# Row halves and banks of the head products and low-rank products in a recurrence's preparation

## The chip, the cores and the metric

One core of one Trainium2 chip runs the whole program. The metric is the device time of one execution in microseconds (us), median over runs.

## The reference

Two layers of a transformer block work on 512 tokens and 256 context tokens of width 1024. Each layer mixes two groups: differential attention over 8 heads, and a gated linear recurrence (RWKV-7) over 8 heads of 64 channels that runs once forwards and once backwards. An output projection and a wide perceptron with a squared ReLU follow. The change touches the inputs of the recurrence. Cut to that:

```python
def direction_terms(k, kk, xw, xa, w0, w_b, a0, a_b, k_a):
    wl = (w0 + jnp.tanh(xw) @ w_b)                      # 64 -> 512, the decay
    decay = jnp.exp(-jnp.exp(-jax.nn.softplus(-wl) - 0.5))
    a = jax.nn.sigmoid(a0 + xa @ a_b)                   # 64 -> 512, the rate
    k_mod = k * (1 + (a - 1) * k_a)
    return decay, k_mod, kk * a

def step(state, inp):
    sa = jnp.einsum("bhvk,bhk->bhv", state, kk_t)
    state = state * w_t - sa * b_t + v_t * k_t
    y = jnp.einsum("bhvk,bhk->bhv", state, r_t)
```

The kernel does not step token by token. It takes chunks of 64 tokens, forms the products of all token pairs of a chunk and head (the tile G below), inverts the triangular part, and carries only a state from chunk to chunk.

## The kernel before, in words

All work is in fp32 or in a split of it into two parts; every fp32 product shows as two records on PE, and every record has a weight load (PEld) that may run beside it. A layer has four stages: the input projection with attention beside it (`phase_wr`), the recurrence, the output projection (`phase_o`) and the perceptron (`phase_f`). The order of instructions on each engine is not the order of the code: a scheduler places each instruction when, by its own reckoning, what it needs is there, a free bank of the matmul accumulator included. On the chip each engine then works through its own list in that fixed order.

The recurrence (line 926 on) goes over six pairs of chunks, n = 0 to 5, each in both directions d, and each with two groups of four heads, pp = 0 and 2. These 24 sets per layer, 48 in all, are prepared by a generator, `preps`, that runs one set ahead with `prep_a`. The first eight sets (n = 0 and 1) are prepared while the attention of the layer ends; the rest between the steps of earlier chunks, beside the products of the step (lines 1186 to 1226) and of the adaptive modulation (line 265, `adar`).

`prep_a` loads the low-rank input (line 970) and r, k and kk (line 973), and multiplies the low-rank input by the two low-rank weights (line 977). The weights for the decay stand in partitions 0 to 63 of `wab`, those for the rate in partitions 64 to 127. The input tile `ltz` is zero except for two diagonal blocks, one in its first 128 columns, one in its last, so that one product 128 rows deep and 256 columns wide gives both halves, next to each other in one bank. Two such products are made per set, and ACT takes a tanh of each quarter (lines 982 and 985).

`prep_b` works on POOL, DVE and ACT through a scaled prefix sum (lines 1014 to 1025) to the tiles BK and KR (lines 1034 to 1038). Two heads share 128 partitions: the even head stands in rows 0 to 63, the odd one in rows 64 to 127. Line 1046 makes the products of a set: first four with the even head's rows into one bank, which DVE multiplies by a mask into G (line 1048), then four with the odd head's rows into the next bank. Then BK is transposed on PE into another bank (line 1053) and copied by ACT (line 1054). After the second group of a direction, a relay of loads by SP (line 1086) carries blocks of G to memory; `inv` loads them in another layout (lines 1115 and 1116), eliminates on POOL for n = 0 and 1 and on DVE after that (lines 1100 and 1102), and the result goes back through memory. `merge` (lines 1152 to 1165) and then `step` follow.

Banks are handed out in turn from a list by `bank` (line 937):

```python
        def bank(shape):
            p = pms.pop(0)
            pms.append(p)
            return p.tile(shape, F32, name=self.n("pb"), tag="m")
```

The list has two banks during the preparation beside the attention, and a third is added when the steps begin (line 1316). A set takes four in turn: one in `prep_a`, two for the products of heads, one for the transposes. A product into a bank waits until its last user has emptied it.

Of the kernel before, what the change touches and what calls it, by code (L numbers as in the profile page):

```python
# [10 lines left out]
F32 = mybir.dt.float32  # L11
F32R = mybir.dt.float32r
AF = mybir.ActivationFunctionType
# [151 lines left out]
class K:  # L165
# [760 lines left out]
    def recurrence(self, l, last, es, side):  # L926

        nc, tc, I, dr = self.nc, self.tc, self.I, self.dr
        tp = self.pool(es, "tp", 1)
# [7 lines left out]
# [5 lines that stand above are left out]
        late = {}  # L942
        wab = pwp.tile([128, 2, 512], F32, name=self.n("wab"))
        nc.sync.dma_start(wab, I["wab"][l].rearrange("d p c -> p d c"))
        ltz = [tp.tile([128, 2, 128], F32, name=self.n("ltz")) for _ in range(2)]

        for z in ltz:
            nc.gpsimd.memset(z, 0.0)
        scm = tp.tile([128, 260], F32, name=self.n("scm"))
        nc.gpsimd.memset(scm, 1.0)  # L950
        nc.gpsimd.memset(scm[:, 0:260:65], 0.0)
# [10 lines left out]
        def prep_a(n, d, pp):  # L962

            need_y = not (last and n < 2)
            tok = slice(tau(n, d) * 128, tau(n, d) * 128 + 128)
            lt = ltz[d]
            if pp == 0:
                for a in range(2):
                    ps = slice(64 * a, 64 * a + 64)
                    nc.sync.dma_start(lt[ps, a, :], self.zd[16, ps, tok])  # L970
            ld = tp.tile([128, 6, 128], F32, name=self.n("ld"), tag="ld", bufs=3)
            j0 = 0 if need_y else 2
            nc.sync.dma_start(ld[:, j0:6, :], self.zd[3 * pp + j0:3 * pp + 6, :, tok].rearrange("j p t -> p j t"))
            pw = bank([128, 2, 2, 128])
            for p in range(2):
                cs = slice((pp + p) * 128, (pp + p) * 128 + 128)
                nc.tensor.matmul(pw[:, p, :, :], wab[:, d, cs], lt, start=True, stop=True, skip_group_check=True)  # L977
            th = tp.tile([128, 2, 128], F32, name=self.n("th"), tag="th", bufs=2)
            ta = tp.tile([128, 2, 128], F32, name=self.n("ta"), tag="ta", bufs=2)
            q = d * 4 + pp  # L980
            for p in range(2):
                nc.scalar.activation(th[:, p, :], pw[:, p, 0, :], AF.Tanh, scale=0.5,
                                     bias=self.Q(l, "w0h")[:, q + p:q + p + 1])
            for p in range(2):
                nc.scalar.activation(ta[:, p, :], pw[:, p, 1, :], AF.Tanh, scale=0.5,
                                     bias=self.Q(l, "a0h")[:, q + p:q + p + 1])
            return ld, th, ta

        def prep_b(n, d, pp, ld, th, ta):
# [12 lines left out]
            KR, BN, G, dcv = sets[(n, d)]  # L1002
            msk = self.mf if d == 0 else self.mb
            nn = 128 if need_y else 64
# [5 lines left out]
            us = slice(2 * pp, 2 * pp + 4)  # L1010
# [28 lines left out]
            nc.gpsimd.tensor_copy(dcv[:, us], ex[:, :, 64 if d == 0 else 0])  # L1039
            yield  # L1040

            for hf in range(2):
                hs = slice(hf * 64, hf * 64 + 64)
                pgt = bank([128, 4, 128])
                for u in range(4):
                    nc.tensor.matmul(pgt[:, u, 0:nn], BK[hs, u, :], KR[hs, 2 * pp + u, 0:nn],  # L1046
                                     start=True, stop=True, skip_group_check=True)
                nc.vector.tensor_tensor(G[:, us, hf, 0:nn], pgt[:, :, 0:nn],
                                        msk[:, 0:nn].unsqueeze(1).to_broadcast([128, 4, nn]), ALU.mult)
            yield  # L1050
            pt = bank([128, 512])
# [685 lines left out]
```

## Time and profile before

| | |
|---|---|
| median of three runs | 2450.8 us (2442.71 to 2458.3) |
| the profiled execution | 2465.64 us |
| its span, first to last instruction | 2463.9 us |
| mean granted clock of PE | 0.933 |
| PE busy | 2273.2 us, 92% |
| recurrence, layer 0, its preparation beside the attention included | from about 376 us to 783 us |
| recurrence, layer 1 | from about 1686 us to 2060 us |

An instruction's row names line, engine, operation and tiles; "64*128" is the part of PE's array used, rows by columns. "Idle before" is time in which the engine waited, with what ended the wait. The chain of waits is followed back from the last instruction, at each step to what released it. The granted clock is a share of PE's full clock: 1.00 is the upper of its two levels, 0.50 the lower. The length of a PE group in the timeline runs to the modelled end of its last record, so the start of the next group tells better how long it held PE.

### The profile page before, as it was taken

The numbers are of one execution on the slowest core, as the hardware profiler recorded it, in microseconds if no ns is written. First come the engines' busy times: TensorE is split into PE (matmuls) and PEld (weight loads), VectorE is DVE, ScalarE is ACT, GpSimd is POOL, SyncE is SP. The second block draws the span as 40 slices with busy tenths as digits, with TensorE's granted clock in tenths as the row PEclk, the third lists the DMA queues.
The fourth block names the chain that finished last, engine by engine and source line by source line (L and its number), as shares of the span: only waits on it lengthen the run. The fifth ranks groups of instructions, "written<-read, shape, count | busy, mean of one in ns | idle before, by whom it ended". The sixth has DMA issues, their size and how long they took to land.

```text
span 2463.9 us, 43744 instructions
## 1 busy us (share of the span) xinstructions
PE 2273.2 (92%) x17150; PEld 1919.2 (78%) x17150; DVE 1516.6 (62%) x2629; ACT 1173.8 (48%) x2393; POOL 806.8 (33%) x1048
## 2 busy tenths in 40 slices
PE   6999998799989999999999989999989978999997
PEld 5887887677768988888888877788767758888886
DVE  5456458558654665555555646657556564778784
ACT  4345547554534543344343535547444444555452
POOL 1212324832111333333330422423641131553530
PEclk8999998798899999999999999999678879999998
DMA  7543535386687422221112354434566663423230
GB/s 270 154 129 94 133 110 140 74 228 172 148 208 236 152 77 69 69 69 61 60 61 85 124 164 122 122 108 115 148 158 158 166 161 137 161 91 117 87 119 35
DMA packets 291630, 313.67 MB, mean 127 GB/s; under 512 B 139680, under 2 KB 220896, under 8 KB 291424
## 3 DMA queue, kind: packets, MB, share of 16 engines
q1 hardware_dynamic: 280320, 284.66, 38.6%
q0 software_dynamic: 10240, 23.08, 5.0%
q8 instruction: 135, 2.21, 0.4%
q10 hardware_dynamic: 864, 3.15, 0.3%
q14 instruction: 71, 0.58, 0.1%
HBM read 257.04 MB, written 53.77 MB: 126 GB/s over the span
## 4 chain that ended last, share of the span: by engine, by line
PE 68%; DMA 10%; DVE 9%; ACT 4%; issue 3%; SPq 2%; POOL 2%; POOLq 0%; DVEq 0%; ACTq 0%
PE pf L351 31%; PE pu L351 15%; PE po L351 4%; DMA raw<-in_ada_w 2%; PE pb L1046 2%; PE po L832 2%; DMA TT<-dt 2%; PE X L1186 1%; PE pb L977 1%; PE adar L265 1%; PE sc L795 1%; DVE wl L1497 1%; PE X L1226 1%; DVE nm L797 1%; PE X L1189 1%
## 5 line engine op out<-in xcount | busy, mean ns | idle before, releaser
L1497 DVE TENSOR_TENSOR wl<-raw,wh 128x1024 fp32r<-128x1024 f32 x170 | 255.8, 1507 | 125.6 <-ACT wh L1496 124.8
L351 PE MATMUL pf<-hl,wh 128*128 128x512 f32 (+1 forms) x832 | 282.1, 342 | 0.0
L351 PE MATMUL pf<-hh,wh 128*128 128x512 f32 (+1 forms) x832 | 280.5, 342 | 0.5 <-ACT hh L397 0.5
L351 PE MATMUL pf<-hh,wl 128*128 128x512 f32 (+1 forms) x832 | 275.7, 342 | 0.0
L1496 ACT ACTIVATE wh<-raw 128x1024 fp32r<-128x1024 f32 x170 | 179.2, 1058 | 162.0 <-PE pf L351 143.9
L351 PE MATMUL pf<-wh,fah 128*128 128x512 f32 x570 | 225.3, 398 | 11.5 <-DVE fu L1630 7.2
L351 PE MATMUL pu<-hh,wh 128*128 128x512 f32 (+1 forms) x632 | 223.5, 354 | 4.8 <-DVE t L557 1.7
L351 PE MATMUL pf<-wl,fah 128*128 128x512 f32 x570 | 225.0, 396 | 0.7 <-DVE wl L1497 0.7
L351 PE MATMUL pf<-wh,fal 128*128 128x512 f32 x570 | 222.8, 397 | 1.8 <-DVE fal L1597 1.8
L351 PE MATMUL pu<-hh,wl 128*128 128x512 f32 (+1 forms) x632 | 218.1, 346 | 4.4 <-DVE wl L340 4.4
L351 PE MATMUL pu<-hl,wh 128*128 128x512 f32 (+1 forms) x632 | 217.8, 345 | 0.0
L797 DVE TENSOR_REDUCE nm<-sc 128x1 f32<-128x768 f32 (+1 forms) x160 | 132.6, 842 | 79.2 <-PE sc L795 78.5
L351 PEld LDWEIGHTS pf<-hl,wh 128*128 128x128 f32 x832 | 156.6, 188 | 20.0 <-DVE hl L399 0.2
L351 PEld LDWEIGHTS pf<-hh,wl 128*128 128x128 f32 x832 | 156.0, 188 | 20.0
L351 PEld LDWEIGHTS pf<-hh,wh 128*128 128x128 f32 x832 | 155.3, 188 | 20.4 <-ACT hh L397 0.8
L799 ACT ACTIVATE e<-sc,nm 128x768 f32<-128x768 f32 (+1 forms) x160 | 130.7, 821 | 53.7 <-DVE nm L797 44.3
L321 POOL TENSOR_TENSOR rs<-ms,pw 128x1 f32<-128x1 f32 (+2 forms) x60 | 56.8, 948 | 286.3 <-DVE ms L319 284.5
L351 PEld LDWEIGHTS pu<-hh,wh 128*128 128x128 f32 x632 | 121.0, 191 | 23.8 <-DVE t L557 2.3
L351 PEld LDWEIGHTS pf<-wh,fah 128*128 128x128 f32 x570 | 107.7, 189 | 38.9 <-ACT fah L1596 13.7
L1630 DVE TENSOR_TENSOR acc<-pf,acc 128x512 f32<-128x512 f32 x155 | 104.2, 682 | 53.9 <-PE pf L351 53.3
L351 PEld LDWEIGHTS pu<-hh,wl 128*128 128x128 f32 x632 | 120.7, 191 | 19.5 <-DVE wl L340 5.3
L351 PEld LDWEIGHTS pu<-hl,wh 128*128 128x128 f32 x632 | 120.8, 191 | 14.2 <-issue 1.7
(262 smaller groups left out, 5644.1 us busy)
## 6 DMA issues: line engine op xcount, KB each, us to landing
raw<-in_w_ff SPq DMA_DIRECT2D x128, 512.0 KB, 3.7
raw<-in_ada_w SPq DMA_DIRECT2D x96, 512.0 KB, 5.8
raw<-in_w_in SPq DMA_DIRECT2D x52, 512.0 KB, 4.6
ld<-zd SPq DMA_DIRECT2D x40, 384.0 KB, 3.9
ks<-qd POOLq DMA_DIRECT2D x64, 192.0 KB, 5.8
zd<-zr SPq DMA_DIRECT2D x22, 384.0 KB
raw<-in_w_out SPq DMA_DIRECT2D x16, 512.0 KB, 5.9
qs<-qd POOLq DMA_DIRECT2D x32, 192.0 KB, 6.0
```

The source lines that it names most:

```text
L265: nc.tensor.matmul(acc[32 * g:32 * g + 32, :], self.sc[:, 2 * kp + k, :], raw[:, k, g * 128:g * 128 + 128], start=(kp + k == 0), stop=(kp ...
L321: nc.gpsimd.tensor_tensor(r, m, self.pw1.to_broadcast([128, cols]), ALU.pow)
L351: nc.tensor.matmul(out, a, b, start=(start and i == 0 and j == 0), stop=(i == n - 1 and j == 2), skip_group_check=not start)
L795: nc.tensor.matmul(sc[:, k0:k1], qs[:, br, tk], ks[:, br, k0:k1], start=True, stop=True)
L797: nc.vector.tensor_reduce(nm, sc, AX.X, ALU.max, negate=True)
L799: nc.scalar.activation(ee, sc, AF.Exp, bias=nm, accum_out=ls[:, br:br + 1])
L832: nc.tensor.matmul(po, pT[:, k * 128:k * 128 + 128], vn[:, k, h * 64:h * 64 + 64], start=(k == 0), stop=(k == nk - 1))
L977: nc.tensor.matmul(pw[:, p, :, :], wab[:, d, cs], lt, start=True, stop=True, skip_group_check=True)
L1046: nc.tensor.matmul(pgt[:, u, 0:nn], BK[hs, u, :], KR[hs, 2 * pp + u, 0:nn], start=True, stop=True, skip_group_check=True)
L1496: nc.scalar.activation(hi, src, AF.Copy)
L1497: nc.vector.tensor_tensor(lo, src, hi.bitcast(F32), sub)
L1630: nc.vector.tensor_tensor(d, p, d, add)
```

## The change

Both kinds of product now go to the two row halves of the array in turn, each half into its own bank.

- The low-rank input loses its zeros: `lt` has 128 columns and comes by one load; the four memsets of `ltz` (two per layer) go. Instead of two products 128 rows deep and 256 columns wide there are four, 64 rows deep and 128 columns wide, half 0 and half 1 in turn, into two banks `pw[0]` and `pw[1]`. The tanh for the decay reads bank 0, that for the rate bank 1.
- The products of heads take both banks first, then go over the four columns u and, inside, over the even and the odd head; both evacuations by DVE stand behind all eight.
- A set takes five banks in turn, not four.

```diff
-        ltz = [tp.tile([128, 2, 128], F32, name=self.n("ltz")) for _ in range(2)]
-
-        for z in ltz:
-            nc.gpsimd.memset(z, 0.0)
+        lts = [tp.tile([128, 128], F32, name=self.n("lt")) for _ in range(2)]
...
-            lt = ltz[d]
+            lt = lts[d]
             if pp == 0:
-                for a in range(2):
-                    ps = slice(64 * a, 64 * a + 64)
-                    nc.sync.dma_start(lt[ps, a, :], self.zd[16, ps, tok])
+                nc.sync.dma_start(lt, self.zd[16, :, tok])
...
-            pw = bank([128, 2, 2, 128])
+
+            pw = [bank([128, 2, 128]) for _ in range(2)]
             for p in range(2):
                 cs = slice((pp + p) * 128, (pp + p) * 128 + 128)
-                nc.tensor.matmul(pw[:, p, :, :], wab[:, d, cs], lt, start=True, stop=True, skip_group_check=True)
+                for a in range(2):
+                    ps = slice(64 * a, 64 * a + 64)
+                    nc.tensor.matmul(pw[a][:, p, :], wab[ps, d, cs], lt[ps, :], start=True, stop=True,
+                                     skip_group_check=True)
...
-                nc.scalar.activation(th[:, p, :], pw[:, p, 0, :], AF.Tanh, scale=0.5,
+                nc.scalar.activation(th[:, p, :], pw[0][:, p, :], AF.Tanh, scale=0.5,
...
-                nc.scalar.activation(ta[:, p, :], pw[:, p, 1, :], AF.Tanh, scale=0.5,
+                nc.scalar.activation(ta[:, p, :], pw[1][:, p, :], AF.Tanh, scale=0.5,
...
+            pgs = [bank([128, 4, 128]) for _ in range(2)]
+            for u in range(4):
+                for hf in range(2):
+                    hs = slice(hf * 64, hf * 64 + 64)
+                    nc.tensor.matmul(pgs[hf][:, u, 0:nn], BK[hs, u, :], KR[hs, 2 * pp + u, 0:nn],
+                                     start=True, stop=True, skip_group_check=True)
             for hf in range(2):
-                hs = slice(hf * 64, hf * 64 + 64)
-                pgt = bank([128, 4, 128])
-                for u in range(4):
-                    nc.tensor.matmul(pgt[:, u, 0:nn], BK[hs, u, :], KR[hs, 2 * pp + u, 0:nn],
-                                     start=True, stop=True, skip_group_check=True)
-                nc.vector.tensor_tensor(G[:, us, hf, 0:nn], pgt[:, :, 0:nn],
+                nc.vector.tensor_tensor(G[:, us, hf, 0:nn], pgs[hf][:, :, 0:nn],
```

The changed lines are 975 (low-rank products) and 1045 (products of heads) in the changed kernel. The scheduler places everything anew, and what it made of the two kinds of product differs from place to place. A number behind `pb` is one bank in one use; rows with the same number and a count are products into the same bank, one behind the other.

PE's list in layer 0, beside the steps of the recurrence (`us` and `X` are products of a step, `adar` of the modulation), before:

```order
L977 MATMUL pb_6166<-ltz_3603,wab_3600 128x256 x2
L1226 MATMUL X_5979<-uv_5975,S_4135 64x64 x6
L1046 MATMUL pb_6205<-S_3914,BK_6199 128x128 x4
L1046 MATMUL pb_6211<-S_3914,BK_6199 128x128 x4
L1210 MATMUL us_5152<-uv_5975,S_4135 64x64 x7
L1053 MATMUL pb_6217<-cst,BK_6199 128x128 x4
```

And the like place after the change:

```order
L1210 MATMUL us_5172<-uv_6005,S_4148 64x64 x5
L1045 MATMUL pb_6243<-S_3922,BK_6237 128x128
L1045 MATMUL pb_6244<-S_3922,BK_6237 128x128
L1045 MATMUL pb_6243<-S_3922,BK_6237 128x128
L1045 MATMUL pb_6244<-S_3922,BK_6237 128x128
L1045 MATMUL pb_6243<-S_3922,BK_6237 128x128
L1045 MATMUL pb_6244<-S_3922,BK_6237 128x128
L1045 MATMUL pb_6243<-S_3922,BK_6237 128x128
L1045 MATMUL pb_6244<-S_3922,BK_6237 128x128
L1210 MATMUL us_5172<-uv_6005,S_4148 64x64 x2
```

Here the eight products of a set alternate between two banks from end to end.

PE's list in layer 0, in the preparation beside the attention (`sc`, `po` and `ptr` are the attention's), before:

```order
L795 MATMUL sc_4576<-ks_3844,qs_3843 128x256
L1046 MATMUL pb_4187<-S_4135,BK_4166 128x128 x4
L1046 MATMUL pb_4193<-S_4135,BK_4166 128x128 x4
L795 MATMUL sc_4583<-ks_3844,qs_3843 128x512
L832 MATMUL po_4542<-vn_572,pT_4494 128x64 x2
```

And after:

```order
L975 MATMUL pb_4011<-lt_3602,wab_3600 128x128 x2
L832 MATMUL po_4496<-vn_572,pT_4455 128x64 x2
L975 MATMUL pb_4012<-lt_3602,wab_3600 128x128 x2
L1045 MATMUL pb_4071<-S_3922,BK_4050 128x128 x4
L795 MATMUL sc_4536<-ks_3849,qs_3848 128x512
L795 MATMUL sc_4536<-ks_3849,qs_3848 128x256
L1045 MATMUL pb_4072<-S_3922,BK_4050 128x128 x4
```

Here neither kind alternates: the four products of the odd heads went behind those of the even heads, with a product of the attention between, and so did the two low-rank halves.

## Rows read from the trace of the kernel before

**Rows 1.** The page, parts 1 and 4: busy time, and the chain by engine
```profile
PE 2273.2 (92%) x17150; PEld 1919.2 (78%) x17150; DVE 1516.6 (62%) x2629; ACT 1173.8 (48%) x2393; POOL 806.8 (33%) x1048
PE 68%; DMA 10%; DVE 9%; ACT 4%; issue 3%; SPq 2%; POOL 2%; POOLq 0%; DVEq 0%; ACTq 0%
```

**Rows 2.** Stretches: length; busy PE, PEld, DVE, ACT, POOL; clock, DMA, GB/s
```profile
376.00:500.00 124.00, 103.31 (x755) 87.72 (x754) 91.68 (x173) 79.42 (x213) 83.23 (x184) 0.81 0.47 114
500.00:700.00 200.00, 183.12 (x2626) 148.21 (x2624) 135.37 (x392) 98.14 (x236) 44.23 (x87) 0.90 0.74 184
1700.00:1950.00 250.00, 225.65 (x2568) 185.66 (x2567) 157.51 (x410) 128.34 (x325) 95.88 (x236) 0.78 0.58 146
```

**Rows 3.** Chain by line: 376:422, 422:495, 495:860, 1640:1815, 1815:2060
```profile
by line: DVE nm L797 12.8%; PE po L832 7.3%; DVE S L1048 6.8%; PE pb L1046 6.6%; ACT e L799 6.1%; PE sc L795 5.9%; issue 5.7%; DVE e L809 5.3%; PE ptr L815 3.8%; DVE th L1031 3.2%; PE pb L977 3.0%; DVE cs L1020 2.8%; ACT pT L818 2.7%; DVE B
by line: DMA W<-da 13.3%; POOL W L1102 10.3%; POOL pr L1100 10.2%; issue 9.0%; PE pb L977 4.7%; DMA TT<-dt 4.4%; PE po L832 4.1%; PE pb L1046 3.7%; POOL rs L321 3.1%; DMA dt<-R 2.9%; DVE S L1048 2.8%; DVE nm L797 2.5%; PE otp L855 2.1%; DVE
by line: PE po L351 15.3%; DMA raw<-in_ada_w 7.4%; DMA TT<-dt 5.4%; PE pb L1046 4.7%; PE X L1226 4.5%; PE adar L265 4.3%; PE pf L351 4.2%; PE X L1186 2.8%; issue 2.7%; DMA raw<-in_w_out 2.6%; DMA S<-gd 2.4%; PE pb L977 2.4%; DMA da<-S 2.3%;
by line: PE pu L351 14.9%; PE pb L1046 10.7%; PE pb L977 6.0%; DMA N<-da 5.9%; issue 4.5%; PE X L1186 4.3%; DVE nm L797 3.6%; PE adar L265 3.4%; PE pb L1053 2.9%; PE po L832 2.9%; PE sc L795 2.6%; POOL pr L1100 2.6%; POOL W L1102 2.3%; PE X
by line: PE X L1186 7.4%; PE po L351 6.5%; DMA TT<-dt 5.8%; issue 5.5%; DMA raw<-in_ada_w 5.3%; PE X L1189 5.2%; PE X L1226 5.1%; DMA S<-zd 4.8%; PE adar L265 4.6%; PE us L1198 4.3%; PE pb L977 3.7%; PE us L1210 3.4%; PE pb L1046 3.3%; DMA 
```

**Rows 4.** Line 1046 alone in two stretches: PE, weight loads
```profile
502.45:502.79 0.34, 0.34 (x3) 0.34 (x4) 1.00 0.73 217
502.79:503.13 0.34, 0.34 (x7) 0.34 (x7) 1.00 1.15 280
```

**Rows 5.** Timeline of PE, lower clock: start, length, group
```profile
1753.49 3.78 PE L1046 MATMUL pb<-S,BK 64*128 64x128 f32 x16
1757.20 1.12 PE L1053 MATMUL pb<-cst,BK 128*128 128x128 f32 x4
1758.25 2.08 PE L1046 MATMUL pb<-S,BK 64*128 64x128 f32 x8
1760.26 1.96 PE L1186 MATMUL X<-uv,S 64*64 64x64 f32 x16
...
1772.43 0.79 PE L1046 MATMUL pb<-S,BK 64*128 64x128 f32 x2
1773.15 1.08 PE L265 MATMUL adar<-raw,sc 128*32 128x128 f32 x16
```

**Rows 6.** Timeline of PE from 502 us, full clock
```profile
502.36 1.71 PE L1046 MATMUL pb<-S,BK 64*128 64x128 f32 x16
504.00 0.66 PE L1053 MATMUL pb<-cst,BK 128*128 128x128 f32 x4
...
505.83 1.13 PE L977 MATMUL pb<-ltz,wab 128*128 128x256 f32 x4
506.89 0.68 PE L1226 MATMUL X<-uv,S 128*64 128x64 f32 x8
...
508.07 0.71 PE L1046 MATMUL pb<-S,BK 64*128 64x128 f32 x4
508.71 0.50 PE L1210 MATMUL us<-uv,S 128*64 128x64 f32 x9
```

**Rows 7.** Line 977: PE's wait, its waiter; line 1053: PE's wait
```profile
  DVE S L1048: 7.0, 7
...
  ACT th L982: 40.1, 36
...
  DVE S L1048: 10.8, 13
```

**Rows 8.** Line 970, loads of the low-rank input: ns min/median/max of an issue
```profile
L970 SPq DMA_DIRECT2D ltz<-zd x48: 444/584/3090, 370.5 to 1892.5; - x48
```

**Rows 9.** Stretches of layer 1, columns as in rows 2
```profile
1740.00:1760.00 20.00, 16.61 (x73) 13.21 (x72) 13.91 (x24) 11.12 (x29) 18.59 (x39) 0.62 0.74 177
1760.00:1780.00 20.00, 20.00 (x126) 15.29 (x125) 5.32 (x9) 4.61 (x11) 8.47 (x21) 0.50 0.52 160
```

## The prediction

> **What bounds the kernel now.** I began with the page: PE is busy for 92% of the span and carries 68% of the chain that ended last, everything else is small beside it [rows 1]. But that is an average over stages of which the change touches two per layer: the preparation beside the end of the attention, and the steps of the recurrence. The busy time by stretch [rows 2] says what these are. From 376 to 500 us DVE has 92 us and POOL 83 us of 124; from 500 to 700 us PE has 183 of 200; from 1700 to 1950 us PE has 226 of 250, at a mean granted clock of 0.78, so that a good part of that stretch ran at the lower of the two levels (1.2 of 2.4 GHz). Next I took the chain of waits stretch by stretch and multiplied its shares out [rows 3]. Line 1046, the products of the heads, has 6.6% of 46 us, 3.7% of 73, 4.7% of 365, 10.7% of 175 and 3.3% of 245, that is 3.0 + 2.7 + 17.2 + 18.7 + 8.1 = 50 us. Line 977, the low-rank products, has 1.4 + 3.4 + 8.8 + 10.5 + 9.1 = 33 us. So 83 us of the path are at stake, 3.4% of the span, and if every one of these products ran at twice its speed with nothing behind it the gain would be 41 us. The reader should keep that figure as the ceiling.
>
> **What two row halves are worth.** The trace already has a place that shows it. Before, the four products of the even heads (rows 0 to 63 of the array) are followed by the four of the odd heads (rows 64 to 127), in another bank. Inside one half three records touch a stretch of 0.34 us; at the border of the halves it is seven [rows 4], so there the two halves do run at the same time. At the lower clock half a set alone (8 records, two to a product) takes 2.01 us, from 1758.25 to 1760.26, and two records 0.72 us, from 1772.43 to 1773.15; both halves one behind the other take 3.71 us, from 1753.49 to 1757.20, and not 4.02 [rows 5]. Six records more for 1.29 us make 0.215 us a record, 0.107 at the full clock. There a whole set takes 1.64 us, from 502.36 to 504.00, a group of four records 0.64 us, from 508.07 to 508.71, and the two low-rank products of a set 1.06 us, from 505.83 to 506.89 [rows 6]. Of the 0.64 us, 0.64 - 4 x 0.107 = 0.21 us are for getting into and out of the group. So half a set alone is 0.21 + 8 x 0.107 = 1.07 us at the full clock, and a set that alternates from end to end 1.07 us too, against 1.64.
>
> **Does the program alternate?** The code does, but the order in which the instructions were built decides, and it follows which bank is free. I counted the whole order of PE. Of 48 sets of head products 12 alternate one by one, 9 stand as four and four without anything between, as before, and 27 stand as four and four with other work between. Before, 29 stood without anything between and 19 apart. Of 48 sets of low-rank products 11 alternate, 7 stand as two and two without a gap, 30 apart; before, 46 were one piece. So a quarter gets what the change describes, and over half loses even the overlap at the border.
>
> **The sum, at the full clock.** Head products before: 29 x 1.64 + 19 x 2 x 1.07 = 88 us. After: 12 x 1.07 + 9 x 1.64 + 27 x 2 x 1.07 = 85 us. Gain 3. Low-rank products before: 48 x 1.06 = 51 us. After, with eight records of half the columns: 11 x 0.64 (four pairs) + 7 x 0.75 (the border overlapped: 5 x 0.107 + 0.21) + 30 x 2 x 0.64 = 51 us. Gain 0. Bounds: with all 48 sets alternating in both, 88 - 48 x 1.07 + 51 - 48 x 0.64 = 57 us of PE time; with nothing overlapping any more, 48 x 2 x 1.07 + 48 x 2 x 0.64 - 139 = 25 us of loss.
> What comes on top, by its place:
> - Changes of shape. The order has 109 stretches of 64-row, 128-column work before and 172 after. The 0.21 us are in the sum, but the first products of whatever comes behind start slower too; I price this at 0.1 us each (half of 0.21), 63 x 0.1 = 6 us, of which PE's half of the path makes +3. Bounds 0 and, at the lower clock throughout, 63 x 0.4 = 25.
> - ACT waits for line 977 36 times, 40.1 us in all [rows 7]. It waits for both halves now; after, the decay's half alone is enough, 0.64 us instead of 1.06. That could give back 48 x 0.42 = 20 us, but only where ACT's result is what DVE and POOL wait for next; I take -4, bounds 0 and -15.
> - Banks. A set takes five allocations now instead of four, over two banks in the preparation and three in the steps. Before, PE stood 10.8 us before line 1053 and 7.0 us before line 977 for DVE to empty a bank [rows 7], about 0.9 us a time. The evacuations themselves (two per set on DVE) stay, and in an alternating set the first starts later, since both banks end together. Behind a waiting product PE holds the attention's scores and the steps' products. I take +2, bounds 0 and +48 x 0.9 x 1/2 = +20.
> - SP issues 24 fewer loads, at a median of 584 ns [rows 8]: 14 us of queue, hardly on the path; -2. The load that remains must bring both halves as before. POOL loses four memsets that stand ahead of its work for the preparation; I price them at nothing.
> - In layer 1 the preparation's sets moved behind attention work and the first steps' products: the eighth set of head products stands 108 other products later than before, the fourth 51. The attention must end anyway, so most of this is exchange; but the elimination for the first chunk starts with the fourth set. I take +2, bounds -5 and +10.
> Sum: -1.5 (half of the 3, since PE has about half of the path there) + 0 + 3 - 4 + 2 - 2 + 2 = -0.5, that is nothing. The profiled execution took 2465.6 us, its span 2463.9, and lies 14.8 us (0.6%) above the median of the runs, so the forecast in the same units is 2466, and 2451 against the median.
>
> **A rule that speaks against the change.** In the rows, a group of 64-row products costs 0.21 us beyond its streaming when it stands among other shapes [rows 6]. The Trainium skill, in "TensorEngine Tiling (Array Packing)", section Key Properties, says that changing the tiling mode, not just the tile, drains TensorE. By that rule the low-rank products, until now 128 rows deep like the attention's work around them, bring a new drain on either side; the trace agrees so far that the cost is there. It is the mechanism of the third rival.
>
> **The rivals.**
> 1. The overlap pays although the order breaks it up, since PE takes work of the other half from further behind, as at the border in rows 4; or the 40 us from 1740 to 1780, where PE was busy for 36.6 us at granted clocks of 0.62 and 0.50 [rows 9], get the full clock because the sets now stand closer together. The first is worth half of the 57 us of PE time, 28; the second 20 x 0.38 + 20 x 0.50 = 18. With both halves of these in part the time is about 2423. For it: rows 4. Against: the other work between the pieces, and that no row here shows the clock rising on such work. Chance 0.2.
> 2. The change does nothing that can be seen, because the scheduler undid it in three quarters of the sets and what is left cancels. This is my forecast, 2451; chance 0.58. Its own range is 2430 to 2472.
> 3. Slower. Place: PE's order in the steps and in layer 1's preparation, where line 977's product is cut in two and each half stands alone between other shapes. Price: 60 new pieces (30 sets, two each) at 0.21 us into and out of a group, doubled where the clock is low, and the 0.1 us behind each: 60 x 0.3 to 60 x 0.6 = 18 to 36 us on the path, if PE is what is waited for at each. It decides when over 0.4 us a piece land there (60 x 0.4 = 24), as in a stretch like 1760 to 1780 us, where PE had no pause at all [rows 9]. Time: 2451 + 29, about 2480. For it: PE's share of the chain [rows 1] and the low clock [rows 2]. Against: in the preparation DVE, not PE, is the fuller engine. Chance 0.22.
>
> **How the numbers follow.** About 1%, 24 us, is what a measurement of this kernel can tell from no change; that makes the borders 2426 and 2475. Faster 0.2, same 0.58, slower 0.22. The range takes in most of both sides: 2415 to 2490.
>
> **What would show it.** Right: the two lines' total share of the chain about as before, near 80 us; alternating sets of 16 records in about 1.1 us; the halves of sets apart at about 1.1 us each; more but shorter waits of ACT for the low-rank products. Wrong, to the faster side: sets that the order holds apart still overlap, or the granted clock between 1740 and 1820 us is 1.0. Wrong, to the slower side: PE standing before lines 975 and 1045 for DVE or ACT for over 20 us in all, or the chain through layer 1's preparation longer by more than 10 us.

## The result, and the profile after the change

The change is slower by a little: median 2466.3 us over 8 runs (2455.35 to 2473.38) against 2445.6 us for the kernel before, run beside it (8 runs, 2441.96 to 2458.3). The ratio is 1.0073, 95% interval 1.0047 to 1.0099, so +12 to +24 us. That lies in the forecast's own range and inside 1%, but it is not the zero that the sum gave.

One trap first. The profiled executions before and after have the same span, 2463.9 us, and whoever lays these two side by side finds no difference to explain. The one of before was a long execution of its kernel (2465.6 us, where its 8 runs here have a median of 2445.6). The kernel before was therefore profiled again (first experiment; span 2441.4 us), and the profile after is read against that one too.

The page of the kernel after, busy time and the chain by engine, beside [rows 1]:

```profile
PE 2293.5 (93%) x17342; PEld 1942.9 (79%) x17342; DVE 1516.6 (62%) x2629; ACT 1176.7 (48%) x2393; POOL 799.3 (32%) x1044
PE 75%; DVE 8%; DMA 6%; ACT 3%; issue 3%; SPq 2%; POOL 2%; ACTq 0%; POOLq 0%; DVEq 0%
```

PE has 192 records more (48 sets, two products more, two records each), and its share of the chain went from 68% to 75%. That share alone is no sign of a loss: in e9 below, which is as fast as the kernel before, it is 75% too. The stretches, beside [rows 2, 9] with the same columns:

```profile
376.00:500.00 124.00, 108.97 (x692) 92.70 (x691) 86.28 (x165) 73.72 (x195) 68.94 (x151) 0.69 0.39 87
500.00:700.00 200.00, 186.51 (x2547) 154.86 (x2547) 137.44 (x398) 100.94 (x244) 56.83 (x120) 0.90 0.72 185
1700.00:1950.00 250.00, 216.94 (x2426) 180.37 (x2426) 141.31 (x363) 118.39 (x296) 92.82 (x231) 0.73 0.57 141
1740.00:1760.00 20.00, 18.52 (x172) 14.68 (x169) 9.28 (x18) 9.74 (x26) 15.99 (x38) 0.75 0.41 130
1760.00:1780.00 20.00, 18.18 (x86) 15.82 (x84) 12.06 (x22) 9.60 (x27) 17.89 (x44) 0.50 0.58 119
```

Fewer records of PE in all three long stretches (692 for 755, 2547 for 2626, 2426 for 2568) say that less is done there by the same time, and the granted clock is lower in the first and the third. In the first stretch that costs nothing: e9 has 697 records and a clock of 0.69 there. The chain by line, from 376 to 860 us and from 1640 to 2100 us:

```profile
by line: PE po L351 13.8%; PE pb L1045 9.4%; PE adar L265 5.2%; PE pb L975 5.0%; PE X L1186 4.5%; PE X L1189 3.9%; PE po L832 3.7%; PE X L1226 3.6%; DMA N<-da 3.6%; issue 3.3%; PE pb L1053 2.9%; PE pf L351 2.9%; PE sc L795 2.5%; PE us L1198
by line: PE po L351 9.4%; PE pb L1045 7.6%; PE pu L351 5.9%; PE adar L265 5.1%; PE X L1186 4.9%; PE pb L975 4.2%; PE X L1189 4.2%; PE po L832 3.5%; issue 2.9%; DVE pr L1100 2.8%; PE X L1226 2.7%; DVE W L1102 2.6%; PE us L1210 2.6%; DMA raw<
```

The two changed lines have 14.4% of 484 us and 11.8% of 460 us, that is 70 + 54 = 124 us of the path, where before they had 83 [rows 3] and in the repeat 72. They did not grow dearer themselves, as the timeline of PE shows (start, length, group; beside [rows 5, 6]):

```profile
426.03 1.16 PE L1045 MATMUL pb<-S,BK 64*128 64x128 f32 x16
...
501.73 1.05 PE L1045 MATMUL pb<-S,BK 64*128 64x128 f32 x8
...
504.99 2.07 PE L1045 MATMUL pb<-S,BK 64*128 64x128 f32 x8 [0.71 <-ACT th L981]
...
1686.81 0.71 PE L975 MATMUL pb<-lt,wab 64*128 64x128 f32 x8
...
1717.63 0.71 PE L975 MATMUL pb<-lt,wab 64*128 64x128 f32 x4
```

A set of heads that alternates takes 1.16 us (1.71 before; 1.64 to the start of the next group), half a set alone 1.05 at the full clock and 2.07 at the lower one, and eight alternating records of the low-rank product cost what four of one half cost, 0.71 us. The waits of PE at line 975 and who waited for that line, then the loads of the low-rank input, beside [rows 7, 8]:

```profile
  DVE S L1048: 8.4, 11
...
  ACT th L981: 21.3, 18
  ACT ta L984: 11.9, 18
```

```profile
L965 SPq DMA_DIRECT2D lt<-zd x24: 319/343/975, 369.0 to 1905.2; - x24
```

PE waits there for a bank 8.4 us instead of 7.0 (7.2 in the repeat). ACT waits for the product 33.2 us, between the 40.1 of the first profile of before and the 27.2 of its repeat, so that no change can be read from it. SP's queue is 48 x 0.584 - 24 x 0.343 = 20 us lighter. Nothing on these lines explains a loss of 18 us. What stands between the sets is the better lead. The timeline of PE after the change, in layer 1 from the fourth set of heads to the eighth (the last line):

```profile
1718.27 1.14 PE L1186 MATMUL X<-uv,S 64*64 64x64 f32 x16
...
1722.10 1.10 PE L1045 MATMUL pb<-S,BK 64*128 64x64 f32 x8
1723.13 0.43 PE L1189 MATMUL X<-sbd,S 128*64 128x128 f32 x2
1723.49 0.41 PE L265 MATMUL adar<-raw,sc 128*32 128x128 f32 x2
...
1724.20 0.43 PE L265 MATMUL adar<-raw,sc 128*32 128x128 f32 x8
1724.55 1.10 PE L1045 MATMUL pb<-S,BK 64*128 64x64 f32 x8
1725.59 0.43 PE L265 MATMUL adar<-raw,sc 128*32 128x128 f32 x8
...
1748.26 1.90 PE L265 MATMUL adar<-raw,sc 128*32 128x128 f32 x26
...
1753.49 1.60 PE L1045 MATMUL pb<-S,BK 64*128 64x64 f32 x16
...
1758.16 2.85 PE L1045 MATMUL pb<-S,BK 64*128 64x64 f32 x16 [0.73 <-ACT th L981]
```

And the eighth set in the repeat of the kernel before:

```profile
1739.26 1.57 PE L1046 MATMUL pb<-S,BK 64*128 64x64 f32 x16 [0.61 <-ACT ta L985]
```

After the change, products of the first two steps (lines 1186, 1189) and of the modulation (line 265) stand among the sets of the preparation. In the kernel before none of them comes ahead of the eighth set. Line 265 alone in two stretches (length, PE, weight loads, clock, DMA share, GB/s), first after the change, then in the repeat of the kernel before:

```profile
1684.00:1758.00 74.00, 8.84 (x128) 4.42 (x128) 0.92 0.52 143
1758.00:1800.00 42.00, 0.00 (x0) 0.00 (x0) 0.50 0.57 110
```

```profile
1684.00:1758.00 74.00, 0.00 (x0) 0.00 (x0) 0.86 0.44 101
1758.00:1800.00 42.00, 5.38 (x128) 3.29 (x128) 0.77 0.69 171
```

The same 128 records, before or behind 1758 us. The eighth set starts 71 us after the layer's first low-rank product (at 1758 us) instead of 55 (at 1739 us). On it wait the relay and the inverse of the second chunk pair, and the products that PE had to run behind it in the kernel before are used up.

### The profile page after: what moved, and what is told of

Same layout as the page of the kernel before. It is cut to its first block, busy times and chain, and to the rows that moved or that the text cites. A ratio compares the mean times of both kernels' runs of the same rounds, so it can differ in the third digit from the quotient of the medians.

```text
span 2463.9 us, 44052 instructions
## 1 busy us (share of the span) xinstructions
PE 2293.5 (93%) x17342; PEld 1942.9 (79%) x17342; DVE 1516.6 (62%) x2629; ACT 1176.7 (48%) x2393; POOL 799.3 (32%) x1044
## 4 chain that ended last, share of the span: by engine, by line
PE 75%; DVE 8%; DMA 6%; ACT 3%; issue 3%; SPq 2%; POOL 2%; ACTq 0%; POOLq 0%; DVEq 0%
PE pf L351 31%; PE pu L351 16%; PE po L351 4%; PE pb L1045 3%; PE po L832 3%; PE adar L265 2%; PE sc L795 2%; PE X L1186 2%; PE pb L975 2%; DMA raw<-in_ada_w 2%; PE X L1189 2%; PE ptr L815 1%; DVE wl L1497 1%; PE X L1226 1%; DMA N<-da 1%
## 5 line engine op out<-in xcount | busy, mean ns | idle before, releaser
L351 PE MATMUL pf<-wh,fah 128*128 128x512 f32 x570 | 224.9, 397 | 11.8 <-DVE fu L1630 7.2
```

What stands on the lines that cost most here:

```text
L351: nc.tensor.matmul(out, a, b, start=(start and i == 0 and j == 0), stop=(i == n - 1 and j == 2), skip_group_check=not start)
```

## The experiments

Theories in turn: A, the cost is in the low-rank product cut into pieces of 64 rows, with more changes of shape on PE; B, it is in the fifth bank; C, any new order of PE is luck; D, formed after the second set of runs, it is in the 104 instructions that PE's order puts ahead of the eighth set of layer 1. A "change of shape" is a place in PE's order where the part of the array in use changes, counted in the order as built; for e10 and e11 it is counted in the trace, where the other kernels show up to 21 more than as built. Times in the last three columns are in us. Layer 0 is counted from its first low-rank product to the first write of its perceptron, layer 1 from its first projection product to the same, in the profiled execution. e1 to e4, e5 to e8 and e9 to e12 ran on three different chips, each group with the kernel before beside it, so the ratios are what can be compared.

| run | median us | ratio to before, 95% interval | changes of shape | X + modulation products ahead of set 8, layer 1 | set 8 after first low-rank product | layer 0 | layer 1 |
|---|---|---|---|---|---|---|---|
| before again (e1) | 2446.6 | 1.0005 (0.9979 to 1.0030) | 601 | 0 | 55 | 468 | 724 |
| the change | 2466.3 | 1.0073 (1.0047 to 1.0099) | 712 | 40 + 64 | 71 | 473 | 742 |
| low-rank part alone (e2) | 2488.2 | 1.0170 (1.0125 to 1.0215) | 723 | 40 + 64 | 76 | 477 | 750 |
| head part alone (e3) | 2439.0 | 0.9956 (0.9928 to 0.9984) | 626 | 0 | 57 | 472 | 722 |
| sets held together (e4) | 2744.8 | 1.1215 (1.1174 to 1.1255) | 602 | 0 | - | - | - |
| five banks, 128 rows (e5) | 2465.5 | 1.0063 (1.0036 to 1.0089) | 638 | 15 + 24 | 70 | 488 | 726 |
| pieces of 128 rows (e6) | 2461.5 | 1.0051 (1.0027 to 1.0075) | 640 | 21 + 24 | 65 | 491 | 722 |
| heads in a chain (e7) | 2450.1 | 1.0005 (0.9982 to 1.0027) | 601 | 0 | 59 | 485 | 715 |
| both in a chain (e8) | 2471.7 | 1.0087 (1.0059 to 1.0114) | 687 | 40 + 64 | 86 | 469 | 753 |
| the change, order held (e9) | 2451.5 | 0.9985 (0.9960 to 1.0011) | 698 | 0 | 59 | 473 | 718 |
| low-rank part, order held (e10) | 2450.2 | 1.0001 (0.9966 to 1.0035) | 705 (trace) | 0 | 63 | 469 | 722 |
| both in a chain, order held (e11) | 2446.1 | 0.9985 (0.9966 to 1.0004) | 679 (trace) | 0 | 75 | 471 | 729 |
| head part alone again (e12) | 2436.5 | 0.9933 (0.9907 to 0.9959) | 626 | 0 | 61 | 464 | 725 |

**e1: the kernel before, once more.** No edit.

> The kernel before, once more, as a control and for a second profile. Both theories: ratio 1.000 within 0.3%. The first profile of the kernel before took 2465.6 us, 20 us above its median; if that execution was merely a long one, this profile lies near 2445 us and shows in which stage the 20 us were, and the granted clock is above 0.933.

Its profile is the one to read against: layer 1 takes 724 us in it, 742 in the first profile of the same kernel. The stretch from 1760 to 1780 us shows where the two part, beside [rows 9]:

```profile
1760.00:1780.00 20.00, 17.23 (x223) 13.31 (x221) 10.28 (x20) 11.65 (x29) 16.24 (x46) 1.00 0.79 213
```

The same instructions in the same order, 223 records at a clock of 1.00 here, 126 at 0.50 there. So one profile can be 18 us off in the time of a layer; verdicts go by the medians.

**e2 and e3: each part alone.** e2 has the diff of lines 945 to 985 alone, e3 that of lines 1042 to 1048:

```diff
-            for hf in range(2):
-                hs = slice(hf * 64, hf * 64 + 64)
-                pgt = bank([128, 4, 128])
...
+            pgs = [bank([128, 4, 128]) for _ in range(2)]
+            for u in range(4):
+                for hf in range(2):
+                    hs = slice(hf * 64, hf * 64 + 64)
```

> Only the low-rank products and their load are changed; the products of heads are as before. Theory A (pieces: the low-rank product is cut in two and each half stands alone among other shapes, 30 new pairs of pieces, 122 more changes of shape in PE's order): slower than before by most of what the whole change costs, +10 to +20 us. Theory B (banks: five allocations a set instead of four): also slower, since five are taken here too, +10 to +20 us. If neither holds, within 5 us of before.

> Only the products of heads are changed; the low-rank products are as before. PE's order alternates from end to end in 18 sets and with a gap in 8, and has only 25 more changes of shape; four banks are taken a set, as before. Theory A: about as before or faster, 0 to -10 us (26 sets x 0.54 us, half of it on the path, is 7 us). Theory B: as before within 5 us, as both banks of the heads are taken at once but no more of them.

The parts go opposite ways: the low-rank part costs 1.7%, some 41 us, the head part gains 0.4%, some 11 us, a little more than the 0 to 10 that theory A gave it. So the loss belongs to the low-rank part, and more of it than the whole change shows. Both theories had expected only 10 to 20 us of the low-rank part, so neither explains the size.

**e4: all 48 sets alternate, each held in one piece.** The whole change, with the scheduler told to place the eight (four) products of a set without anything between them:

```diff
+            with tc.tile_critical():
+                for u in range(4):
...
```

> The whole change, and the eight products of heads and the four low-rank products of a set are held together when the order is made, so that all 48 sets of both alternate from end to end; the order has as many changes of shape as before (602 against 601). Theory A: PE has 57 us less work at the full clock, half of it on the path: 15 to 30 us faster than before. Theory B: five banks a set and both halves waited for at once: not faster than before, +5 to +20 us, with PE waiting longer for DVE and ACT ahead of the products.

12% slower, where theory A expected a gain of 15 to 30 us. The waits from 376 to 900 us (who, for whom, us in total, times, longest):

```profile
DVE S L1050 <- PEq L1043: 88.4, 22, 12.2
ACT th L982 <- PEq L971: 77.2, 24, 7.9
PEld pb L976 <- issue: 74.1, 24, 6.9
PEld pb L1047 <- issue: 62.1, 24, 7.9
```

At each of the 24 sets of layer 0 PE's weight loads stand some 3 us ahead of either group (74.1 / 24, 62.1 / 24) for nothing else that the profile shows, 136 us in all, in a layer 0 of 619 us instead of 468, and DVE and ACT wait for PE's sequencer (PEq) at the group's border. Holding a set together puts waits of its own at its border, so the run says nothing about alternation.

**e5 and e6: the bank and the pieces, without 64-row pieces.** e5 gives each of the two whole low-rank products its own bank. e6 keeps the zeros and the two loads and cuts the product by columns:

```diff
-            pw = bank([128, 2, 2, 128])
+            pw = [bank([128, 2, 128]) for _ in range(2)]
...
-                nc.tensor.matmul(pw[:, p, :, :], wab[:, d, cs], lt, start=True, stop=True, skip_group_check=True)
+                for a in range(2):
+                    nc.tensor.matmul(pw[a][:, p, :], wab[:, d, cs], lt[:, a, :], start=True, stop=True,
+                                     skip_group_check=True)
```

> The kernel before, with one edit: the two low-rank products of a set, still one piece each of 128 rows by 256 columns with the zeros, go to a bank each, so that a set of the preparation takes five banks of the pool in place of four, and 24 of the 48 pairs come to stand apart in TensorE's order (638 changes of shape in place of 601). No product is cut and none has 64 rows of input more than before. Theory A (the 41 us of the low-rank part alone come from the product cut in pieces of 64 rows, and from the 723 changes of shape): within 5 us of the kernel before. Theory B (they come from the fifth bank, for which a set's second product waits, so that the preparation is later and ScalarE's tanh with it): slower by 15 to 40 us, with the eighth set of both layers 5 to 15 us later than in the repeat of the kernel before (444 and 1739 us). Theory C (TensorE's order is only luck where it changes at all): anything from -15 to +40 us, with no relation to the time of the eighth set.

> The low-rank part alone, but on 128 rows: the zeros and the two loads stay as before, and the product is cut in two pieces of 128 columns that go to two banks, so that a set has four pieces over five banks as in the low-rank part alone, with 640 changes of shape in place of 723 and no piece of 64 rows. Theory A: close to the kernel before, within 8 us (a piece more a set is 96 times some 0.2 us at most beside other work, the changes of shape are gone). Theory B: slower by 15 to 40 us, as with the fifth bank alone. If the fifth bank alone costs nothing and this one costs 30 us or more, the pieces themselves are the cost and not their shape.

+0.6% and +0.5%: theory A expected next to nothing here, so it falls as the whole story. The size, 15 and 12 us, is at the lower end of what B asked for, but the place is not B's: layer 1 takes 726 and 722 us, as in the kernel before, and the loss is in layer 0, 488 and 491 us for 468, in its later steps. From 700 to 760 us in e5, then from 700 to 740 us in the repeat of the kernel before:

```profile
700.00:720.00 20.00, 15.42 (x268) 12.48 (x261) 12.28 (x45) 3.92 (x9) 0.12 (x1) 0.51 0.54 114
720.00:740.00 20.00, 16.11 (x255) 13.57 (x254) 5.09 (x9) 7.54 (x18) 2.27 (x2) 0.66 0.73 180
740.00:760.00 20.00, 19.80 (x201) 15.09 (x203) 10.73 (x23) 8.54 (x20) 6.55 (x6) 0.66 0.71 209
```

```profile
700.00:720.00 20.00, 17.75 (x275) 14.65 (x274) 11.17 (x31) 9.08 (x19) 4.34 (x5) 1.00 0.79 193
720.00:740.00 20.00, 14.64 (x276) 10.46 (x275) 8.98 (x13) 8.07 (x19) 7.68 (x6) 0.83 0.96 262
```

The last steps of the layer run in e5 at a granted clock of 0.51 to 0.66 instead of 0.83 to 1.00. What brings that about is not shown. The change itself does not lose there (473 us).

**e7 and e8: alternation by order alone.** Each product is issued behind the one before it, so that it alternates without being held in one piece (here the odd head comes first); e7 for the heads alone, e8 for both kinds:

```diff
+                    with ExitStack() as behind:
+                        if mm is not None:
+                            behind.enter_context(tc.issue_after(mm.ins))
+                        mm = nc.tensor.matmul(pgs[hf][:, u, 0:nn], BK[hs, u, :], KR[hs, 2 * pp + u, 0:nn],
+                                              start=True, stop=True, skip_group_check=True)
```

> The head products alone, with each of the eight of a set issued after the one before it in alternation, so that all 48 sets alternate (32 in one piece, 16 with other work between two of their products) and the number of changes of shape stays at 601. The low-rank product is as before. Four of the five banks as before, no fifth. Theory A and theory B both: faster than the kernel before by 0 to 20 us, since the 26 alternating sets of the head part alone gave 11 us and 48 are 1.8 times as many; what 48 alternating sets can save of PE's path is 48 times 0.57 us = 27 us at most. Theory C: no relation to the number of alternating sets, -15 to +30 us.

> The whole change, with the pieces of both products issued in alternation: all 48 sets of either alternate (34 and 32 in one piece), 687 changes of shape (601 before, 712 in the change). Theory A (pieces of 64 rows and changes of shape): between the change and the kernel before, +5 to +15 us, since a quarter of the added changes goes. Theory B (the fifth bank): as slow as the change or slower by up to 10, +15 to +30 us, and 20 to 40 us behind the head part alone in alternation. If it is faster than the kernel before, the pieces that stand apart were the cost, and neither the shape nor the bank.

With all 48 sets of heads alternating, e7 is level with the kernel before, while e3 with 26 was faster: the number of alternating sets does not set the time, and the gain of up to 20 us that both theories expected did not come. It has the shortest layer 1 of the runs so far (715 us) and a layer 0 as long as those of e5 and e6 (485 us). e8 loses 0.9%, some 21 us, as theory B expected, all of it in layer 1 (753 us). At this point the table's fifth column sorts layer 1: 40 + 64 products ahead of the eighth set in the three kernels that take 742 to 753 us, none or some 40 in those that take 715 to 726. That is theory D. The table alone only suggests it, since the first profile of before took 742 us with none ahead; the next runs put it to the test.

**e9, e10 and e11: the order held.** Products of the first two steps and of the modulation are issued behind the last head product of the eighth set, in layer 1 alone; no other line is touched. e9 does it to the change, e10 to the low-rank part, e11 to e8:

```diff
+            if l == 1 and (n, d, pp) == (1, 1, 2):
+                late["set8"] = mm.ins
...
+                    with ExitStack() as behind:
+                        if n < 1 and "set8" in late:
+                            behind.enter_context(tc.issue_after(late["set8"]))
+                        nc.tensor.matmul(X[0:w, h * 64:h * 64 + 64], s["G"][64:128, h - h % 2 + q, h % 2, 0:w],
...
+                                if n < 1 and "set8" in late:
+                                    behind.enter_context(tc.issue_after(late["set8"]))
                                 ada(ADA[l])
```

> The whole change, with one order forced in layer 1: the products of the first step into X (line 1186) and the modulation products (line 265) are issued behind the last head product of the eighth set, as TensorE has them in the kernel before. In the change 40 and 64 of these instructions (208 records) stand ahead of that product, in the kernel before none. Nothing else is edited: five banks, row halves, pieces and loads stay (698 changes of shape, 712 in the change). Theory D (the cost is in what TensorE's order puts ahead of the eighth set of layer 1, whose relay the inverse waits for): the eighth set comes 10 to 16 us sooner after the first low-rank product than in the change (71 us there, 55 in the repeat of the kernel before), layer 1 from its first projection to its perceptron takes 715 to 730 us (741 in the change, 725 before), and the time is 10 to 20 us below the change, so within 8 us of the kernel before. Theories A (shape of the low-rank pieces) and B (the fifth bank): both are still there, so within 5 us of the change, +15 to +20 us.

> The low-rank part alone, with the same order forced in layer 1 as in the run before this one (there too 40 and 64 instructions stand ahead of the eighth set; here none). Theory D: 15 to 30 us below the low-rank part alone (which was +41 us against the kernel before), layer 1 from first projection to perceptron 720 to 732 us in place of 750. Theories A and B: within 6 us of the low-rank part alone. If it gains less than 15 us, order explains only a part, and the row halves of the low-rank product keep the rest.

> The whole change with both products issued in alternation, and the same order forced in layer 1 (104 instructions stood ahead of the eighth set without it, none with it). Theory D: 12 to 28 us below the same kernel without the forced order (+21 us against the kernel before), so -7 to +9 us, layer 1 in 720 to 732 us in place of 753. Theories A and B: within 6 us of it.

All three come back to the kernel before: ratios of 0.9985, 1.0001 and 0.9985, from 1.0073, 1.0170 and 1.0087. Taken by the ratios, that gives back 0.88%, 1.69% and 1.02%, 22, 41 and 25 us; for the low-rank part that is more than the 15 to 30 us expected. Row halves, pieces, the fifth bank and the single load are still there (698 changes of shape in e9, 601 before), so A and B fall for what they claimed of the change. The traces agree on the place: PE's records come in the same order in the change and in e9 up to the first product that was held, layer 0 included, but for two swaps of neighbours. The timeline of e9 shows the eighth set with the step's products behind it, from 1746 us:

```profile
1745.93 2.85 PE L1045 MATMUL pb<-S,BK 64*128 64x64 f32 x16 [0.51 <-ACT th L981]
1748.71 1.96 PE L1191 MATMUL X<-uv,S 64*64 64x64 f32 x16
...
1753.55 1.54 PE L265 MATMUL adar<-raw,sc 128*32 128x128 f32 x48
```

The products that were held run there and in the next 40 us. Line 265 alone in e9, for the two stretches that were shown for the change and for before:

```profile
1684.00:1758.00 74.00, 1.54 (x48) 1.27 (x48) 0.82 0.46 119
1758.00:1800.00 42.00, 5.08 (x80) 2.84 (x80) 0.73 0.69 162
```

What PE gets done behind the eighth set, first in the change (its row from 1760 us was shown above), then in e9:

```profile
1780.00:1800.00 20.00, 14.92 (x178) 12.67 (x176) 8.77 (x17) 8.82 (x23) 14.54 (x41) 0.50 0.57 99
1800.00:1820.00 20.00, 10.48 (x119) 9.08 (x120) 15.97 (x46) 4.25 (x10) 14.02 (x37) 0.54 0.31 91
1820.00:1840.00 20.00, 12.36 (x253) 10.07 (x251) 8.21 (x28) 6.57 (x12) 0.90 (x5) 0.63 0.77 151
```

```profile
1760.00:1780.00 20.00, 15.30 (x124) 11.81 (x122) 8.43 (x16) 7.58 (x19) 13.17 (x37) 0.66 0.69 197
1780.00:1800.00 20.00, 16.07 (x267) 13.12 (x265) 11.01 (x22) 11.13 (x30) 15.20 (x40) 0.78 0.65 122
1800.00:1820.00 20.00, 13.38 (x178) 11.13 (x178) 17.92 (x54) 5.95 (x12) 12.22 (x33) 0.71 0.56 167
1820.00:1840.00 20.00, 18.56 (x324) 14.95 (x324) 14.15 (x39) 15.61 (x40) 6.22 (x16) 1.00 0.74 176
```

From 1760 to 1840 us PE gets through 86 + 178 + 119 + 253 = 636 records in the change, at clocks of 0.50 to 0.63, and through 893 in e9, at 0.66 to 1.00. In the last 40 us of these it is busy for 22.8 us and 31.9 us. None of the held products is left by then in either kernel, so they do not fill that pause themselves. Nor does the picture prove the cause: the first profile of the kernel before, with none of the products ahead, has only 754 records in the same 80 us and the same 742 us of layer 1. The evidence is in the medians of the held runs.

The lateness of the eighth set does not explain the loss either. In e11 it comes 75 us after the first low-rank product, later than in the change, and nothing is lost; in layer 0 of the change it comes after 88 us instead of 70, and that layer takes 473 us (470 and 468 in the two profiles of before). The first product of the second merge, which needs the inverse, starts 144 us after the first low-rank product in the change, 139 in e9 and 149 in e11. So what is shown is that the order costs the time; by which wait it does so is not shown.

More rode along than the 104 products: behind the first of them the scheduler placed the rest of layer 1 anew, and PE's records come in another order at about a hundred places between the change and e9. One of these could matter. In the change the head products of the fourteenth set stand behind the second merge, and this merge waits for a transfer (PE's waits from 1820 to 1835 us):

```profile
PE pg L1152 <- DMA TT<-dt: 6.1, 1, 6.1
```

There the fourteenth set follows the thirteenth after 32 us, in e9 after 10. The held order undid that too, so e9 alone cannot say which of the two cost the time. Other kernels speak to it, though not on the change itself: e3 and e12, which are one program, have that gap (28 and 29 us) and lose nothing, e8 has a short one (14 us) and loses 0.9%. That speaks for the products ahead of the eighth set. The other places were not tested one by one.

**e12: the head part once more.** The same edit as e3. It ran half an hour after e3, on another chip; the "another day" below is not so.

> The head part alone once more, as it was run first, on another day of the chip: no X or modulation product stands ahead of the eighth set of layer 1 in its order. If the 11 us that it gained were real, it is again 5 to 15 us below the kernel before; if they were the chance of that set of runs, within 4 us of it. All theories allow both; this run says whether the head part is worth keeping.

0.9933 (0.9907 to 0.9959), after 0.9956: a gain of 11 and 16 us, below both kernels. It is the version to keep. Where the gain comes from is not settled: its profile (span 2439.4 us) differs little from the repeat of before (2441.4 us), which is among the shortest executions of that kernel, and e7 says that more alternation does not add to it.

## Why the prediction was right or wrong

- **What bounds the kernel, and the ceiling.** Right as far as it went. Of the 83 us of path at stake none became free; the path's share of the two lines rose to 124 us instead of "about as before, near 80 us". The sign was a poor one: the share is 72 us in the repeat of before and 96 us in e9, and these two take the same time.
- **Row halves.** Right. An alternating set was put at 1.07 us and takes 1.16 to the modelled end of its last record; half a set was put at 1.07 and takes 1.05. The Trainium skill says in "TensorEngine Tiling (Array Packing)", section Key Properties, that tiles operate independently; the 0.71 us for eight alternating records, the price of four, agree.
- **The sum over the order of the products.** That the scheduler breaks up three quarters of the sets was counted before any run, and the gain from the rest was rightly put near nothing. That alternation everywhere would bring something is not borne out: 48 sets in e7 gave a ratio of 1.0005.
- **ACT, SP and the banks.** ACT's wait, from which -4 us was taken for the path, is 33.2 us after the change and 40.1 and 27.2 us in the two profiles of before; the term was read from one profile and cannot be told from its spread. SP's queue fell by 20 us where 14 were expected; PE's wait at line 975 for DVE to empty a bank rose by 1.4 us where +2 was taken. The runs of the held order show that all of these together come to nothing that can be measured: 0.9985 with an interval of 0.9960 to 1.0011.
- **The step that failed: the moved sets of layer 1.** The prediction counted it, "the eighth set of head products stands 108 other products later than before, the fourth 51", and took +2 with bounds of -5 and +10, because "The attention must end anyway, so most of this is exchange". For the eighth set it was not exchange with the attention: 40 + 64 = 104 products of the first two steps and of the modulation now stand ahead of it, which ran behind it before. Layer 1 took 742 us instead of the repeat's 724, and forcing the order gave back 22 us by the ratios. The term was some +20, twice the upper bound. Which wait on PE's path carries it stays open, and it is not the lateness of the eighth set, 16 us here, since e11 and layer 0 show sets as late without a loss. I looked at the fourth set, which starts the first elimination, where in the trace 23 of the products that moved ahead are the attention's and 17 are not, and did not ask what the 108 ahead of the eighth were.
- **The third rival**, that cutting the low-rank product costs by drains at changes of shape, named the right part for the wrong reason. The low-rank part alone did cost 41 us, more than the 29 given to that rival. But with the order held it keeps its pieces, with some 700 changes of shape (601 before), and has a ratio of 1.0001. A net price of a change of shape, whatever its drain, cannot be seen here.
- **The first rival**, a faster kernel through overlap: the head part alone is faster (-0.4 and -0.7%), by 11 to 16 of the 28 us that the rival was given. That the overlap does it is not shown, since more of it in e7 gained nothing.
- **What would show it.** Of the two signs for the slower side, the first (PE standing before lines 975 and 1045 for DVE or ACT for over 20 us) did not appear, though only just: 19 us with the weight loads, 12 before. The second (layer 1's preparation longer by over 10 us) did not appear as worded: from the first low-rank product to the first merge it is 106 us, 97 in the repeat and 109 in the profile that the prediction read.
- **Luck.** The forecast of 2451 us had a range of its own to 2472, and 2466 lies in it. But the sum missed a term of some 20 us, and that this stays inside 1% is luck: the low-rank part alone, without the head part's gain, takes 2488 us, outside the range.

What stays open: why the scheduler, given a low-rank product in pieces, places the steps ahead of the preparation; by which wait that order costs the time, and whether the kernel before would lose as much if the 104 products were forced ahead in it, which no run does; the 17 to 23 us that e5, e6 and e7 lose in layer 0; and the source of the head part's gain.

## What to carry to other kernels

When a scheduler places everything anew, compare what stands ahead of the last preparation of a stage, name the kinds of work that moved there, and ask what the engine is left with behind it; an edit that costs nothing in itself can cost its whole loss through the order, and here one forced order gave it back. Test a change's parts alone, and then with the old order forced, before the edit is blamed. Profile the kernel before more than once: two executions of it differed by as much as the effect sought.

## What the runs showed of the hardware that was not expected

- One program with one order varies more than most effects here: the runs of the kernel before beside the last group, but for one of 35, span 2437.4 to 2463.1 us. Its two profiles differ in layer 1 by 18 us, and the difference shows at 1760 to 1780 us, where one was granted 1.00 of the clock and the other 0.50 with PE busy for all 20 us [rows 9].
- The second row half comes almost for nothing: 16 alternating records of 64 rows take 1.16 us, 8 of one half 1.05.
